# The pool of split weights opened after the pools of small tiles and activations

## The chip, the core and the metric

The program runs on one core of a Trainium2 chip. The metric is device time in microseconds (us) of one execution. The time of a kernel is the median of its timed runs; beside them stands one execution that was recorded by the profiler.

## What is computed

Two layers of a decoder trunk over 256 tokens of width 2048, in fp32. Layer 0 mixes by multi-head latent attention and a causal pooling mixer, layer 1 by a gated short convolution; each is followed by a squared-ReLU MLP of hidden width 8192.

```
for layer in range(2):
    h = rmsnorm(x, mix_norm_g[layer])
    if layer == 0:
        c_q, c_kv, k_rope, u_pool = split(h @ even_w_in)
        a = mla(c_q, c_kv, k_rope, ...)          # 8 heads, causal softmax
        b = pool_mixer(u_pool, ...)              # trailing means over 2/4/8/16 tokens
        x = x + concat([a, b]) @ even_w_out
    else:
        gate_b, gate_c, u = split(h @ odd_w_in)
        x = x + (gate_b * conv3(gate_c * u)) @ odd_w_out
    x = x + square(relu(rmsnorm(x, mlp_norm_g[layer]) @ w_mlp_up[layer])) @ w_mlp_down[layer]
```

## The kernel before

The weights come from HBM piece by piece, and every large product runs on TensorE. To keep fp32 accuracy with TensorE's fp32r operands, each weight and each activation is split in two halves, hi (the value rounded to fp32r) and lo (the rest), and a product is summed from hi·hi, hi·lo and lo·hi.

**The weights' way.** `slab` (L124) loads a piece of 1 MB, 128 partitions by 4 k-tiles by 512 columns, into a tile of the pool `raws` by a DMA that SyncE issues (L129). `halved` (L132) then cuts it into pieces of two k-tiles; for each, ScalarE writes the hi half (L141) and VectorE subtracts it from the raw weight and writes the lo half (L142). Both go to the pool `halves`, under the tags `hi` and `lo`, six buffers each, taken in turn. TensorE reads them in one of two roles: `columns_out` (L161, L162) has them as the stationary operand and streams the normed input `xT` past them, with 512 columns for hi and 256 for lo; `tokens_out` (L154 to L156) and the seven-product form of the MLP's second matrix (`down_seven`, L777 to L779) have an activation tile as the stationary operand and stream 512 columns of hi or lo.

**The activations.** `acts` holds four buffers of 8 KB a partition under the tag `hT` (`act_tile`); they carry the attention's and the MLP's activations, hi and lo, and at the start two of them, named `x0T`, hold the transposed input. The pool `small` has the short-lived tiles of VectorE and ScalarE: four buffers of 2 KB under the tag `t` (named junk, h, c, cu, b, y and so on), one named `f`, and statistics of a few bytes. `down_seven` also uses sums of activations, named `fT` by the profile, which lie in a pool of the MLP stage.

**Where pools lie.** A pool is a fixed stretch of each partition's on-chip memory (SBUF). The pools are stacked: each begins where the one opened before it ends, so the order in which they are opened sets the addresses. `const` and `big` are opened first, then the three pools of the change, then the pools of a stage (`raws` and others, through `new_stage`, L77). The attention's pool is stacked from the other end. The order of the instructions on each engine is that of the program text; the waits follow from which tiles an instruction reads and writes, and from which buffers are taken again.

```
    pools = dict(halves=ctx.enter_context(tc.tile_pool(name="halves", bufs=6)))
    small = ctx.enter_context(tc.tile_pool(name="small", bufs=2))
    T4 = dict(tag="t", bufs=4)
    acts = ctx.enter_context(tc.tile_pool(name="acts", bufs=4))
```

Of the kernel before, what the change touches and what calls it, by code (L numbers as in the profile page):

```python
# [67 lines left out]
def trunk(ctx: ExitStack, tc, x_in, xT_in, gains_in, pos_in, w_up, w_down, w_in, pool_in, w_uq, w_ukv,  # L68
# [16 lines left out]
                for name, bufs in wanted.items():  # L85
                    pools[name] = stage[-1].enter_context(tc.tile_pool(name=uid(name), bufs=bufs, reuse_waits="tile"))

    pools = dict(halves=ctx.enter_context(tc.tile_pool(name="halves", bufs=6)))
    small = ctx.enter_context(tc.tile_pool(name="small", bufs=2))
    T4 = dict(tag="t", bufs=4)  # L90
    acts = ctx.enter_context(tc.tile_pool(name="acts", bufs=4))
    psum = ctx.enter_context(tc.tile_pool(name="psum", bufs=4, space=PSUM))

    count = [0]
# [910 lines left out]
```

## Time and profile before

| | us |
|---|---|
| median of 3 runs (2029.35 to 2031.46) | 2030.74 |
| the profiled execution | 2031.15 |
| its span, first to last instruction | 2029.4 |
| TensorE (PE) matmuls busy in it | 2018.0 |
| VectorE (DVE) busy | 1395.3 |
| ScalarE (ACT) busy | 1120.8 |
| GpSimd (POOL) busy | 96.7 |

The 1.75 us between the profiled execution and its span lie around the first and the last instruction. In the profile's rows L161 is line 161 of the kernel, "ps<-xT,hi" names what an instruction writes and reads, PEld is TensorE's load of a stationary operand, and an engine's idle time is put down to what ended it.

### The profile page before, as it was taken

The numbers are of one execution on the slowest core, as the hardware profiler recorded it, in microseconds if no ns is written. First come the engines' busy times: TensorE is split into PE (matmuls) and PEld (weight loads), VectorE is DVE, ScalarE is ACT, GpSimd is POOL, SyncE is SP. The second block draws the span as 40 slices with busy tenths as digits, with TensorE's granted clock in tenths as the row PEclk, the third lists the DMA queues.
The fourth block names the chain that finished last, engine by engine and source line by source line (L and its number), as shares of the span: only waits on it lengthen the run. The fifth ranks groups of instructions, "written<-read, shape, count | busy, mean of one in ns | idle before, by whom it ended". The sixth has DMA issues, their size and how long they took to land.

```text
span 2029.4 us, 26720 instructions
## 1 busy us (share of the span) xinstructions
PE 2018.0 (99%) x10532; PEld 1722.8 (85%) x10532; DVE 1395.3 (69%) x1737; ACT 1120.8 (55%) x1480; POOL 96.7 (5%) x126
## 2 busy tenths in 40 slices
PE   8999999999999999999999999999999999999999
PEld 8987888888888888888888888888888888888887
DVE  6677567776777777676566656567776677767774
ACT  6576556655556555555444444456555565555552
POOL 1330000000000000000000000000000000000000
PEclk9999999999999999999999999999999999999999
DMA  8453758788878878665555557658797987879663
GB/s 316 157 203 130 241 179 237 256 251 262 272 236 265 256 239 270 230 208 187 184 184 188 186 185 242 213 177 248 236 282 245 274 235 260 257 250 283 197 216 124
DMA packets 67006, 459.72 MB, mean 227 GB/s; under 512 B 7280, under 2 KB 9760, under 8 KB 11968
## 3 DMA queue, kind: packets, MB, share of 16 engines
q1 hardware_dynamic: 58224, 397.89, 54.4%
q0 software_dynamic: 8224, 58.94, 15.3%
q8 instruction: 82, 1.34, 0.3%
q10 hardware_dynamic: 432, 1.18, 0.2%
q14 instruction: 44, 0.36, 0.0%
HBM read 455.89 MB, written 2.10 MB: 226 GB/s over the span
## 4 chain that ended last, share of the span: by engine, by line
PE 95%; DVE 1%; POOL 1%; DMA 1%; ACT 1%; issue 0%; ACTq 0%; DVEq 0%; POOLq 0%
PE ps L161 32%; PE ps L162 16%; PE ps L156 10%; PE ps L154 10%; PE ps L155 10%; PE ps L779 4%; PE ps L777 4%; PE ps L778 4%; POOL pn L489 1%; DVE lo L142 1%; PE ps L289 1%; DMA raw<-in_even_w_in 1%; ACT hi L141 0%; PE ps L618 0%; DMA raw<-in_even_w_out 0%
## 5 line engine op out<-in xcount | busy, mean ns | idle before, releaser
L142 DVE TENSOR_TENSOR lo<-raw,hi 128x1024 fp32r<-128x1024 f32 (+2 forms) x694 | 847.8, 1225 | 450.5 <-ACT hi L141 449.9
L141 ACT CAST hi<-raw 128x1024 fp32r<-128x1024 f32 (+2 forms) x694 | 724.2, 1046 | 620.7 <-PE ps L161 355.7
L161 PE MATMUL ps<-xT,hi 128*128 128x512 f32 x2816 | 997.3, 398 | 0.0
L162 PE MATMUL ps<-xT,lo 128*128 128x256 f32 x2816 | 790.5, 281 | 0.0
L161 PEld LDWEIGHTS ps<-xT,hi 128*128 128x128 f32 x2816 | 528.9, 188 | 129.4
L162 PEld LDWEIGHTS ps<-xT,lo 128*128 128x128 f32 x2816 | 532.0, 189 | 4.0
L154 PE MATMUL ps<-hi,hT 128*128 128x512 f32 (+1 forms) x896 | 351.3, 392 | 0.0
L156 PE MATMUL ps<-hi,hT 128*128 128x512 f32 (+1 forms) x896 | 350.3, 391 | 0.0
L155 PE MATMUL ps<-lo,hT 128*128 128x512 f32 (+1 forms) x896 | 348.0, 388 | 0.0
L156 PEld LDWEIGHTS ps<-hi,hT 128*128 128x128 f32 x896 | 168.4, 188 | 36.5
L155 PEld LDWEIGHTS ps<-lo,hT 128*128 128x128 f32 x896 | 168.3, 188 | 36.1
L154 PEld LDWEIGHTS ps<-hi,hT 128*128 128x128 f32 x896 | 168.4, 188 | 35.5 <-issue 1.3
L141 ACT CAST hi<-t 128x1024 fp32r<-128x1024 f32 x84 | 88.2, 1050 | 98.7 <-PE ps L161 51.5
L142 DVE TENSOR_TENSOR lo<-t,hi 128x1024 fp32r<-128x1024 f32 x84 | 102.6, 1222 | 46.3 <-ACT hi L141 45.3
L767 POOL DMA_DIRECT2D t<-in_w_mlp_down x42 | 36.7, 874 | 1153.6 <-DVE lo L142 746.6
L779 PE MATMUL ps<-hi,fT 128*128 128x512 f32 x224 | 88.0, 393 | 0.0
L778 PE MATMUL ps<-lo,fT 128*128 128x512 f32 x224 | 87.8, 392 | 0.0
L777 PE MATMUL ps<-hi,fT 128*128 128x512 f32 x224 | 87.7, 391 | 0.0
L779 PE MATMUL ps<-hi,hT 128*128 128x512 f32 x168 | 66.2, 394 | 0.0
L777 PE MATMUL ps<-hi,hT 128*128 128x512 f32 x168 | 65.9, 392 | 0.0
L778 PE MATMUL ps<-lo,hT 128*128 128x512 f32 x168 | 65.6, 391 | 0.0
L867 DVE SCALAR_TENSOR_TENSOR x<-ps,r,x 128x512 f32<-128x512 f32 (+1 forms) x73 | 50.9, 737 | 14.8 <-PE ps L156 14.8
(184 smaller groups left out, 1562.7 us busy)
## 6 DMA issues: line engine op xcount, KB each, us to landing
raw<-in_w_mlp_up SPq DMA_DIRECT2D x128, 1024.0 KB, 6.1
raw<-in_w_mlp_down SPq DMA_DIRECT2D x114, 1024.0 KB, 5.1
raw<-in_odd_w_in SPq DMA_DIRECT2D x48, 1024.0 KB, 4.9
t<-in_w_mlp_down POOLq DMA_DIRECT2D x42, 1024.0 KB, 9.4
raw<-in_even_w_out SPq DMA_DIRECT2D x16, 1024.0 KB, 5.0
raw<-in_odd_w_out SPq DMA_DIRECT2D x16, 1024.0 KB, 4.9
t<-in_w_mlp_down SPq DMA_DIRECT2D x14, 1024.0 KB, 4.8
v<-in_w_mlp_down SPq DMA_DIRECT2D x14, 1024.0 KB, 4.9
```

The costliest lines, as they stand in the source:

```text
L141: a = nc.scalar.copy(h, r)
L142: v = nc.vector.tensor_tensor(out=l, in0=r, in1=h.bitcast(F32), op=ALU.subtract)
L154: nc.tensor.matmul(o, lhsT=a_hi, rhs=hi[:, c0:c0 + n], start=first, stop=False)
L155: nc.tensor.matmul(o, lhsT=a_hi, rhs=lo[:, c0:c0 + n], start=False, stop=False)
L156: nc.tensor.matmul(o, lhsT=a_lo, rhs=hi[:, c0:c0 + n], start=False, stop=last)
L161: nc.tensor.matmul(o, lhsT=hi[:, c0:c0 + P], rhs=act[:, kt, :], start=first, stop=False)
L162: nc.tensor.matmul(o[:, S:2 * S], lhsT=lo[:, c0:c0 + P], rhs=act[:, kt, 0:S], start=False, stop=last)
L767: nc.gpsimd.dma_start(b, at(e, n), accum_op=ALU.add)
L777: nc.tensor.matmul(o, lhsT=a_hi, rhs=hi, start=q == 0, stop=False)
L778: nc.tensor.matmul(o, lhsT=a_hi, rhs=lo, start=False, stop=False)
L779: nc.tensor.matmul(o, lhsT=a_lo, rhs=hi, start=False, stop=q == 3)
L867: nc.vector.scalar_tensor_tensor(out=xb, in0=ps[:, t, :n], scalar=r2[0][:, t:t + 1], in1=xb, op0=ALU.mult, op1=ALU.add)
```

## The change

The line that opens `halves` moves behind the two that open `small` and `acts`.

```
-    pools = dict(halves=ctx.enter_context(tc.tile_pool(name="halves", bufs=6)))
     small = ctx.enter_context(tc.tile_pool(name="small", bufs=2))
     T4 = dict(tag="t", bufs=4)
     acts = ctx.enter_context(tc.tile_pool(name="acts", bufs=4))
+    pools = dict(halves=ctx.enter_context(tc.tile_pool(name="halves", bufs=6)))
     psum = ctx.enter_context(tc.tile_pool(name="psum", bufs=4, space=PSUM))
```

The sizes of the three pools stay, so the stretch that they fill together, bytes 67,360 to 163,039 of each partition, stays too, and with it every pool behind it. The built programs have the same instructions, in the same order on each of the five engines, with the same waits. Only the start addresses of the tiles in these three pools differ:

| pool | bytes a partition | starts at, before | starts at, after |
|---|---|---|---|
| `big`: the normed input xT (its last 32 KB) | 32,768 | 34,592 | 34,592 |
| `halves`: six hi | 26,112 | 67,360 | 110,816 |
| `halves`: six lo | 26,112 | 93,472 | 136,928 |
| `small` | 10,688 | 119,584 | 67,360 |
| `acts`: four hT | 32,768 | 130,272 | 78,048 |
| `raws` (first pool of a stage) | 24,576 | 163,040 | 163,040 |
| MLP stage: fT | 16,384 | 204,000 | 204,000 |

`halves` moves up by 43,456 bytes, `small` and `acts` move down by 52,224. All starts before and after are multiples of 32, and both distances are multiples of 64.

More of the change, by code (lines that the diff above doesn't have):

```diff
@@ L86, in new_stage @@
                     pools[name] = stage[-1].enter_context(tc.tile_pool(name=uid(name), bufs=bufs, reuse_waits="tile"))
-    pools = dict(halves=ctx.enter_context(tc.tile_pool(name="halves", bufs=6)))
     small = ctx.enter_context(tc.tile_pool(name="small", bufs=2))
@@ L91, in trunk @@
     acts = ctx.enter_context(tc.tile_pool(name="acts", bufs=4))
+    pools = dict(halves=ctx.enter_context(tc.tile_pool(name="halves", bufs=6)))
     psum = ctx.enter_context(tc.tile_pool(name="psum", bufs=4, space=PSUM))
```

## The prediction

> **What bounds the kernel now.** I read the page's busy times first, then the waits of TensorE alone, then busy time by stretch, and last the groups of instructions with shapes kept apart, for what a matmul, a split or a subtraction takes at different addresses. The first row is from the page, the next six are all the waits that the trace finds on PE, with total us, times and longest.
>
> ```profile
> PE 2018.0 (99%) x10532; PEld 1722.8 (85%) x10532; DVE 1395.3 (69%) x1737; ACT 1120.8 (55%) x1480; POOL 96.7 (5%) x126
> ...
> PE ps L154 <- ACT hi L141: 2.6, 1, 2.6
> PE ps L255 <- POOL ident masks.py:199: 2.5, 1, 2.5
> PE ps L610 <- DVE hT L205: 1.1, 1, 1.1
> PE ps L155 <- DVE lo L142: 0.9, 1, 0.9
> PE ps L167 <- ACT qkv L525: 0.4, 1, 0.4
> PE ps L167 <- DVE hT L205: 0.3, 1, 0.3
> ```
>
> Of the span of 2029.4 us the matmuls fill 2018.0. The waits sum to 7.8 us, 2.5 of them ahead of the first instruction; what is left of the 11.4, some 3.6 us, lies behind the last matmul. So TensorE streams without a break, and two things alone can move the end: the pace of the matmuls themselves, or another engine that becomes so slow that TensorE waits for it. Rows of busy time by stretch say how far off the second is. Their columns are us, then busy us and instructions of PE, PEld, DVE, ACT and POOL, then clock, DMA share and GB/s. The first row is the end of the latent projection, the second a piece of the first MLP, the third of the convolution's input product; the row below them counts L142 alone in the MLP piece.
>
> ```profile
> 20.00:60.00 40.00, 40.00 (x244) 40.00 (x243) 33.02 (x84) 26.45 (x43) 0.79 (x1) 1.00 0.76 286
> ...
> 400.00:600.00 200.00, 200.00 (x1014) 169.25 (x1013) 146.38 (x169) 114.13 (x130) 7.88 (x9) 1.00 0.81 253
> ...
> 980.00:1180.00 200.00, 200.00 (x1134) 173.33 (x1133) 124.90 (x150) 87.67 (x96) 0.62 (x6) 1.00 0.53 184
> ...
> 400.00:600.00 200.00, 108.22 (x90) 1.00 0.81 253
> ```
>
> PE is busy for all of each stretch, at a granted clock of 1.00. In the MLP, DVE has 53.6 us idle of 200 beside 90 subtractions of L142, so each could take 0.6 us more, 1.8 us in place of 1.2, before DVE filled the stretch.
>
> **The change, part by part.** It removes no instruction, adds none, moves none past another on any engine or DMA queue, and adds or takes no wait: the instruction lists of the two builds agree row for row. What changes is where the buffers of three pools lie: six hi, six lo, four hT and the small tiles. So the sum has one term for each kind of access to a moved buffer, the number of accesses times whatever the new address adds, and the question is whether an address has a price. The trace of before can answer that, since it has like instructions on buffers far apart. First TensorE, grouped with shapes kept apart (count, busy us, mean ns of one):
>
> ```profile
> L161 PE MATMUL ps<-xT,hi 128*128 128x512 f32 x2816 | 997.3, 398 | 0.0
> L162 PE MATMUL ps<-xT,lo 128*128 128x256 f32 x2816 | 790.5, 281 | 0.0
> ...
> L779 PE MATMUL ps<-hi,fT 128*128 128x512 f32 x224 | 88.0, 393 | 0.0
> L778 PE MATMUL ps<-lo,fT 128*128 128x512 f32 x224 | 87.8, 392 | 0.0
> L777 PE MATMUL ps<-hi,fT 128*128 128x512 f32 x224 | 87.7, 391 | 0.0
> L779 PE MATMUL ps<-hi,hT 128*128 128x512 f32 x168 | 66.2, 394 | 0.0
> L777 PE MATMUL ps<-hi,hT 128*128 128x512 f32 x168 | 65.9, 392 | 0.0
> L778 PE MATMUL ps<-lo,hT 128*128 128x512 f32 x168 | 65.6, 391 | 0.0
> ```
>
> Lines 777 to 779 run the same three matmuls with two different stationary tiles. hT lies at 130,272 to 163,039, fT at 204,000 to 220,383. Over all three lines fT takes (87.7+87.8+88.0)/672 = 392.1 ns and hT (65.9+65.6+66.2)/504 = 392.3 ns: 0.15 ns apart for a move of at least 41 KB, where the change moves hT by 52. The busy sums are rounded to 0.1 us, which blurs that by about as much again. The streamed operand shows the same: hi at 67,360 (L777) and lo at 93,472 (L778) are read at 391 to 392 ns. The loads of the stationary operand don't differ either, whether it is hi, hT or fT:
>
> ```profile
> L161 PEld LDWEIGHTS ps<-xT,hi 128*128 128x128 f32 x2816 | 528.9, 188 | 129.4
> ...
> L777 PEld LDWEIGHTS ps<-hi,fT 128*128 128x128 f32 x224 | 42.0, 188 | 9.9
> ...
> L777 PEld LDWEIGHTS ps<-hi,hT 128*128 128x128 f32 x168 | 31.5, 188 | 7.3 <-ACT hT L200 0.4
> ```
>
> Most places that are new for one kind of tile were used by PE before, for the other kind: the four hT come to 78,048 to 110,815, where hi and lo buffers stood, and all of lo comes to where hT stood. I take 0 for TensorE, and as bounds 0.3 ns to either side for each of the 10,532 matmuls (the 0.15 and its blur): 3.2 us less to 3.2 us more.
>
> Now the engines that write the buffers. ACT's split and DVE's subtraction, by source tile, and their writes to hT beside those to fT:
>
> ```profile
> L141 ACT CAST hi<-raw 128x1024 fp32r<-128x1024 f32 x676 | 707.0, 1048 | 607.7 <-PE ps L161 355.7 <-PE ps L156 123.7 <-PE ps L779 56.3
> ...
> L141 ACT CAST hi<-v 128x1024 fp32r<-128x1024 f32 x28 | 29.4, 1048 | 43.2 <-PE ps L161 23.5 <-DVE lo L142 19.7
> ...
> L200 ACT CAST hT<-h 128x512 fp32r<-128x512 f32 x64 | 39.7, 620 | 0.6
> ...
> L200 ACT CAST fT<-f 128x512 fp32r<-128x512 f32 x56 | 34.6, 618 | 9.6 <-DVE f L748 9.6
> ...
> L142 DVE TENSOR_TENSOR lo<-raw,hi 128x1024 fp32r<-128x1024 f32 x676 | 827.3, 1226 | 435.8 <-ACT hi L141 435.2
> ...
> L142 DVE TENSOR_TENSOR lo<-v,hi 128x1024 fp32r<-128x1024 f32 x28 | 34.3, 1225 | 33.9 <-ACT hi L141 33.9
> ...
> L201 DVE TENSOR_TENSOR hT<-h,hT 128x512 fp32r<-128x512 f32 x64 | 44.0, 687 | 1.1 <-ACT hT L200 0.7
> ...
> L201 DVE TENSOR_TENSOR fT<-f,fT 128x512 fp32r<-128x512 f32 x56 | 38.4, 685 | 0.0
> ```
>
> The largest difference by place is 2 ns in 600 or 700. Even if all 1,737 instructions of DVE took 2 ns more, that is 3.5 us spread over 2029, beside an idle time of 0.6 us at each subtraction, and ACT waits for PE far longer (607.7 us ahead of L141). Cost 0, covered by the matmuls; with no idle time to cover it, it would be those 3.5 us at most.
>
> One kind of DMA has a moved target, the loads of the transposed input into x0T at the start; what waited for them stands at the end of the row of their only reader on ACT:
>
> ```profile
> L204 ACT ACTIVATE xT<-x0T,gains 128x256 fp32r<-128x256 f32 x16 | 7.0, 498 | 1.0 <-DMA gains<-in_gains 0.8 <-DMA x0T<-in_xT 0.2
> ```
>
> They write the same bytes at another offset, and 0.2 us of waiting is put down to them; I take 0, with 0.2 us more or less as bounds. The DMAs into `raws`, all others of weight, have the targets they had.
>
> The sum: 2031.15 (the profiled execution: 2029.4 of span and 1.75 around it) + 0 = 2031.15 us. That execution is 0.41 us above the median of the runs, 2030.74, so the forecast in terms of a median is **2030.7 us**.
>
> The rows say that PE is not held up by what ACT, DVE and the DMAs do in the same memory: 200.00 us busy of 200.00 in an MLP stretch where they are busy for 114, 146 and 81%. The Trainium skill, in "SBUF — State Buffer", section "Who interferes with whom", has a rule of the same tenor: PE and ACT have ports of their own and never wait on anyone, the one shared pair of ports is that of DVE and GpSimd, and nothing in it goes by address along a partition. By that rule the first two rivals below would be worth 0 and the sum would stay 2031.15. The page speaks of ports, not of what lies behind them, so I leave the rivals some chance.
>
> **The rivals.**
>
> *Slower, by neighbours.* PE reads its stationary and its streamed operand at once. Suppose that costs more when the two lie close. After the change hT ends at 110,816, just where the hi buffers begin; before, 10.7 KB lay between lo's end and hT's start and 36.8 KB between hi's end and hT's. The nearest row for such a neighbourhood is L161: in it xT, which ends at 67,360, streams past hi, which before begins there, and it takes 398 ns against 391 for L777. If those 7 ns were the price and passed to the matmuls of hT with hi or lo (L154 to L156 with 896 each, L777 to L779 with 168 each, 3,192 in all), the time would be 2030.7 + 22.3 = **2053 us**. It decides from 4.1 us/3,192 = 1.3 ns a matmul, since PE has nothing to hide it under. Against it: hT and fT, at least 10 and 84 KB above the halves, differ by 0.15 ns; and L161 differs from L777 in other ways, as every second matmul there is a short one.
>
> *Faster, by the same mechanism.* L161 loses the neighbour: between xT and hi lie 43 KB after. If its 398 ns fell to 391, 2,816 × 7 = 19.7 us would go, to **2011 us**. Against it: the spread over all buffers and k-tiles of the other half of the pair, L162, is narrow. The row gives count, then min, median and max in ns:
>
> ```profile
> L162 PE MATMUL ps<-xT,lo x2816: 276/281/285, 270.8 to 1970.3; 128*128 128x256 f32 x188
> ```
>
> xT's nearest and farthest k-tile lie 30 KB apart and lo's buffers 22 KB, and all pairings together stay within 9 ns.
>
> *Slower, by DVE.* The lo buffers come to end at 163,040, where `raws` begins, and L142 reads one and writes the other. It decides from 1.8 us, where DVE fills the MLP. If neighbours doubled it, to 2.45 us, the 676 pieces read from raw would cost 827 us more; DVE has 2029.4 − 1395.3 = 634 us idle in all, so at least 193 us would be added, for **2224 us** or more. Against it: raw at 163,040 and v at 195,808 are read at the same 1225 to 1226 ns.
>
> *The change moves nothing.* If the allocator gave the same addresses, the time would be the same; the built addresses do differ, so it has no share of its own.
>
> **How the numbers follow.** No change: 0.88. Slower by neighbours: 0.06; slower by DVE: 0.01. Faster: 0.05. About 0.2%, 4.1 us, is what a measurement of this kernel can tell from no change, and the bound of 3.2 us stays inside it; so the chances are 0.05 faster, 0.88 the same, 0.07 slower. The range takes the bounds of 3.2 us and the spread of the runs around their median, 1.4 below and 0.7 above: 2030.7 − 4.6 = 2026.1 to 2030.7 + 3.9 = 2034.6. It leaves out the rivals, 0.12, and some of the rest.
>
> **What would show it.** L161 and L162 stay at 398 and 281 ns, L777 to L779 at 391 to 394 with both stationary tiles, the stationary loads at 188, L141 at 1048 and L142 at 1226, and PE's waits at about 8 us in the same six places. A matmul group of hT alone that is 1.3 ns or more longer shows the first rival; L161 alone shorter shows the second; new waits of PE for L142 show the third. If all groups are as before and the time still moved by more than 4 us, the argument that an address acts only through the length of the instructions is wrong.

## The result, and the profile after

| | before | after |
|---|---|---|
| median of 5 runs, us | 2030.18 (2029.35 to 2031.46) | 2018.58 (2017.77 to 2020.08) |
| ratio to before, 95% interval | | 0.9943 (0.9931 to 0.9954) |
| profiled execution, us | 2031.15 | 2020.08 |
| its span, us | 2029.4 | 2018.3 |
| PE matmuls busy, us | 2018.0 | 2007.2 |

The kernel became faster by 11.6 us, where no change was forecast. The forecast's range ended at 2026.1. The profile after, first the page's busy times, then all waits of PE:

```profile
PE 2007.2 (99%) x10532; PEld 1723.4 (85%) x10532; DVE 1394.9 (69%) x1737; ACT 1122.2 (56%) x1480; POOL 96.4 (5%) x126
...
PE ps L255 <- POOL ident masks.py:199: 2.5, 1, 2.5
PE ps L154 <- ACT hi L141: 2.0, 2, 1.1
PE ps L167 <- ACT qkv L525: 1.6, 1, 1.6
PE ps L155 <- DVE lo L142: 1.0, 2, 0.9
PE ps L167 <- DVE hT L205: 0.2, 1, 0.2
```

The waits sum to 7.3 us, as good as the 7.8 of before. The span lost 11.1 us and PE's busy time lost 10.8: TensorE still streams from end to end, it only needs less time for the same 10,532 matmuls. The granted clock doesn't explain that: it was 0.999 before and 0.998 after. The groups say which (count, busy us, mean ns of one):

```profile
L161 PE MATMUL ps<-xT,hi 128*128 128x512 f32 x2816 | 992.1, 394 | 0.0
L162 PE MATMUL ps<-xT,lo 128*128 128x256 f32 x2816 | 790.8, 281 | 0.0
L154 PE MATMUL ps<-hi,hT 128*128 128x512 f32 x880 | 344.6, 392 | 0.0
L156 PE MATMUL ps<-hi,hT 128*128 128x512 f32 x880 | 342.8, 390 | 0.0
L155 PE MATMUL ps<-lo,hT 128*128 128x512 f32 x880 | 342.5, 389 | 0.0
L777 PE MATMUL ps<-hi,fT 128*128 128x512 f32 x224 | 88.1, 393 | 0.0
L779 PE MATMUL ps<-hi,fT 128*128 128x512 f32 x224 | 87.7, 392 | 0.0
L778 PE MATMUL ps<-lo,fT 128*128 128x512 f32 x224 | 87.0, 389 | 0.0
L777 PE MATMUL ps<-hi,hT 128*128 128x512 f32 x168 | 65.8, 392 | 0.0
L779 PE MATMUL ps<-hi,hT 128*128 128x512 f32 x168 | 65.5, 390 | 0.0
L778 PE MATMUL ps<-lo,hT 128*128 128x512 f32 x168 | 65.4, 389 | 0.0
```

A row's busy time counts overlapping matmuls once. Every L161 begins before the last L161 has ended, so its busy time runs through: it is the length of the whole stream of pairs L161 and L162, and L162's isn't to be added. That stream is 5.2 us shorter (997.3 to 992.1). Before, the x880 rows of the three lines were 346.8, 345.8 and 343.5:

```profile
L154 PE MATMUL ps<-hi,hT 128*128 128x512 f32 x880 | 346.8, 394 | 0.0
L156 PE MATMUL ps<-hi,hT 128*128 128x512 f32 x880 | 345.8, 393 | 0.0
L155 PE MATMUL ps<-lo,hT 128*128 128x512 f32 x880 | 343.5, 390 | 0.0
```

So L154 to L156 went from 1036.1 to 1029.9, 6.2 us less, and L777 to L779 lost 0.7 (fT) and 1.0 (hT). That sums to 13.1 us; the span lost 11.1, as some small groups moved the other way and neighbouring groups overlap. The pace didn't change everywhere, though. L161 has 1,024 pairs in each MLP and 768 in the convolution's input product. Here are its rows in the first MLP (260 to 930 us) and in the convolution (930 to 1280 us), before and then after:

```profile
L161 PE MATMUL ps<-xT,hi 128*128 128x512 f32 x1024 | 362.9, 397 | 0.0
...
L161 PE MATMUL ps<-xT,hi 128*128 128x512 f32 x768 | 271.6, 399 | 0.0
```

```profile
L161 PE MATMUL ps<-xT,hi 128*128 128x512 f32 x1024 | 360.3, 394 | 0.0
...
L161 PE MATMUL ps<-xT,hi 128*128 128x512 f32 x768 | 271.6, 396 | 0.0
```

The second MLP has the rows of the first, 362.9 and 360.3. So the whole gain on pairs lies in the MLPs, 2.6 us in each, and the convolution's pairs take 271.6 us as before. DVE and ACT work as they did:

```profile
L142 DVE TENSOR_TENSOR lo<-raw,hi 128x1024 fp32r<-128x1024 f32 x676 | 827.1, 1226 | 429.1 <-ACT hi L141 428.3
...
L141 ACT CAST hi<-raw 128x1024 fp32r<-128x1024 f32 x676 | 708.3, 1050 | 599.7 <-PE ps L161 338.1 <-PE ps L156 115.2 <-PE ps L779 54.6
```

### The profile page after: what moved, and what is told of

Its sections match the earlier page's. It is cut to its first block, busy times and chain, and to the rows that moved or that the text cites. A ratio compares the mean times of both kernels' runs of the same rounds, so it can differ in the third digit from the quotient of the medians.

```text
span 2018.3 us, 26720 instructions
## 1 busy us (share of the span) xinstructions
PE 2007.2 (99%) x10532; PEld 1723.4 (85%) x10532; DVE 1394.9 (69%) x1737; ACT 1122.2 (56%) x1480; POOL 96.4 (5%) x126
## 4 chain that ended last, share of the span: by engine, by line
PE 96%; DVE 1%; POOL 1%; DMA 1%; ACT 1%; issue 0%; SPq 0%; ACTq 0%; DVEq 0%; POOLq 0%
PE ps L161 32%; PE ps L162 16%; PE ps L154 10%; PE ps L156 10%; PE ps L155 10%; PE ps L777 4%; PE ps L779 4%; PE ps L778 4%; DVE lo L142 1%; DMA raw<-in_even_w_in 1%; PE ps L289 1%; PE ps L167 0%; PE ps L169 0%; PE ps L168 0%; POOL pn L489 0%
## 5 line engine op out<-in xcount | busy, mean ns | idle before, releaser
L142 DVE TENSOR_TENSOR lo<-raw,hi 128x1024 fp32r<-128x1024 f32 (+2 forms) x694 | 847.6, 1225 | 444.4 <-ACT hi L141 443.5
L141 ACT CAST hi<-raw 128x1024 fp32r<-128x1024 f32 (+2 forms) x694 | 725.7, 1048 | 613.2 <-PE ps L161 338.1
L161 PE MATMUL ps<-xT,hi 128*128 128x512 f32 x2816 | 992.1, 394 | 0.0
L162 PE MATMUL ps<-xT,lo 128*128 128x256 f32 x2816 | 790.8, 281 | 0.0
L161 PEld LDWEIGHTS ps<-xT,hi 128*128 128x128 f32 x2816 | 529.4, 188 | 123.8
L162 PEld LDWEIGHTS ps<-xT,lo 128*128 128x128 f32 x2816 | 528.0, 188 | 3.6
L154 PE MATMUL ps<-hi,hT 128*128 128x512 f32 (+1 forms) x896 | 349.1, 390 | 0.0
L156 PE MATMUL ps<-hi,hT 128*128 128x512 f32 (+1 forms) x896 | 347.3, 388 | 0.0
L155 PE MATMUL ps<-lo,hT 128*128 128x512 f32 (+1 forms) x896 | 347.1, 387 | 0.0
L154 PEld LDWEIGHTS ps<-hi,hT 128*128 128x128 f32 x896 | 168.3, 188 | 35.0 <-issue 1.3
L156 PEld LDWEIGHTS ps<-hi,hT 128*128 128x128 f32 x896 | 168.3, 188 | 34.8
L155 PEld LDWEIGHTS ps<-lo,hT 128*128 128x128 f32 x896 | 168.4, 188 | 33.2
L141 ACT CAST hi<-t 128x1024 fp32r<-128x1024 f32 x84 | 88.5, 1053 | 92.7 <-PE ps L161 50.7
L142 DVE TENSOR_TENSOR lo<-t,hi 128x1024 fp32r<-128x1024 f32 x84 | 102.6, 1221 | 44.3 <-ACT hi L141 44.1
L777 PE MATMUL ps<-hi,fT 128*128 128x512 f32 x224 | 88.1, 393 | 0.0
L779 PE MATMUL ps<-hi,fT 128*128 128x512 f32 x224 | 87.7, 392 | 0.0
L777 PE MATMUL ps<-hi,hT 128*128 128x512 f32 x168 | 65.8, 392 | 0.0
L779 PE MATMUL ps<-hi,hT 128*128 128x512 f32 x168 | 65.5, 390 | 0.0
```

Of the source, the lines that this page charges most:

```text
L141: a = nc.scalar.copy(h, r)
L142: v = nc.vector.tensor_tensor(out=l, in0=r, in1=h.bitcast(F32), op=ALU.subtract)
L154: nc.tensor.matmul(o, lhsT=a_hi, rhs=hi[:, c0:c0 + n], start=first, stop=False)
L155: nc.tensor.matmul(o, lhsT=a_hi, rhs=lo[:, c0:c0 + n], start=False, stop=False)
L156: nc.tensor.matmul(o, lhsT=a_lo, rhs=hi[:, c0:c0 + n], start=False, stop=last)
L161: nc.tensor.matmul(o, lhsT=hi[:, c0:c0 + P], rhs=act[:, kt, :], start=first, stop=False)
```

## The experiments

Three theories, all on the length of matmuls. **Alignment**: what counts is the distance between the tile that PE streams and the stationary tile, modulo some power of two. Modulo 256 bytes, hi lay 0 above xT before and lies 192 above it after; against hT the distance was 64 and is 0; against fT also 64 and 0. **Place**: what counts is the gap in bytes, as in the prediction's first two rivals. **History**: PE's pace can settle in more than one way, and any disturbance tips it.

Fifteen kernels ran, all but one with the instructions of before in the same order, and only addresses changed, by another order of the pools or by unused bytes ("pad") between them. The table gives distances modulo 256, the median time, the busy time of L161, and the sums of the x880 rows of L154 to L156 and of the x224 rows of L777 to L779. (The expectations of the later runs count the short forms of L154 to L156 in, which adds 13.5 us: 1049.6 before, 1043.4 after.) The kernel of before, run beside them, had medians of 2029.4 to 2030.2.

| kernel | hi−xT | hi−hT | hi−fT | us | L161 | L154–156 | L777–779, fT |
|---|---|---|---|---|---|---|---|
| before | 0 | 64 | 64 | 2030.2 | 997.3 | 1036.1 | 263.5 |
| after | 192 | 0 | 0 | 2018.6 | 992.1 | 1029.9 | 262.8 |
| small, halves, acts | 192 | 0 | 0 | 2018.5 | 992.2 | 1029.9 | 262.9 |
| halves, acts, small | 0 | 0 | 64 | 2023.3 | 994.1 | 1029.9 | 263.5 |
| before, 192 in front | 192 | 64 | 64 | 2032.2 | 999.2 | 1035.4 | 263.8 |
| before, 256 in front | 0 | 64 | 64 | 2029.7 | 992.6 | 1035.3 | 263.5 |
| before, 64 ahead of acts | 0 | 0 | 0 | 2020.5 | 994.2 | 1029.6 | 263.0 |
| after, 64 in front | 0 | 0 | 0 | 2021.0 | 994.1 | 1029.6 | 263.0 |
| after, 128 in front | 64 | 0 | 0 | 2025.6 | 999.2 | 1029.9 | 263.2 |
| after, 32 in front | 224 | 0 | 0 | 2007.7 | 982.6 | 1029.9 | 262.4 |
| after, 32 ahead of halves | 224 | 32 | 0 | 2025.1 | 982.6 | 1044.3 | 262.5 |
| before, 224 in front, 32 ahead of acts | 224 | 32 | 32 | 2028.5 | 982.6 | 1044.3 | 264.7 |
| after, 32 in front, 32 between hi and lo | 224 (lo 0) | 0 (lo 32) | 224 (lo 0) | 2029.2 | 985.4 | 1044.2 | 265.1 |
| after, 96 in front | 32 | 0 | 0 | 2014.9 | 988.2 | 1030.2 | 263.4 |
| before, 224 in front, 64 ahead of acts | 224 | 0 | 0 | 2007.3 | 982.6 | 1029.9 | 262.4 |
| after, 160 in front | 96 | 0 | 0 | 2007.2 | 982.1 | 1029.6 | 261.8 |

The three right columns come from one profiled execution. At hi−xT 0 that was a long one for before and a short one for the four others; **By stage**, below, says what that makes of L161.

**Other orders.** The first kernel opens small, then halves, then acts:

```
     small = ...
+    pools = dict(halves=...)
     acts = ...
```

> Order small, halves, acts: acts and hT lie where they did before (130,272), halves start at 78,048. Alignment theory (what counts is the distance between the two operands of a matmul modulo 256 bytes: hi to xT was 0 and is 192 after the change, hi to hT was 64 and is 0 after it): both distances are here as after the change, so the time is 2018 to 2020 us, the busy sum of L161 and L162 about 1783 us as after (before 1788), that of L154 to L156 with hT about 1030 (before 1036). Place theory (the gap in bytes between tiles): the gap from xT to hi is 10,688 instead of 43,456 and the gap from lo to hT is 0, so L154 to L156 are not faster than before and the time stays above 2024 us. History theory (a small disturbance tips the pace of the matmul stream): any time from 2018 to 2031.

The profile of that kernel, its groups as above:

```profile
L161 PE MATMUL ps<-xT,hi 128*128 128x512 f32 x2816 | 992.2, 394 | 0.0
...
L154 PE MATMUL ps<-hi,hT 128*128 128x512 f32 x880 | 344.6, 392 | 0.0
L156 PE MATMUL ps<-hi,hT 128*128 128x512 f32 x880 | 342.8, 390 | 0.0
L155 PE MATMUL ps<-lo,hT 128*128 128x512 f32 x880 | 342.5, 389 | 0.0
```

With other places and gaps but the distances of after, it has the rows of after to 0.1 us, and the time (2018.5). Place is out for this pair, alignment is met. The second opens halves, acts, small:

```
     pools = dict(halves=...)
+    acts = ...
     small = ...
-    acts = ...
```

> Order halves, acts, small: halves stay where they were before, hT moves down by 10,688 bytes to 119,584. Alignment theory: hi to xT modulo 256 is 0 as before, so L161 and L162 keep their sum of 1788 us; hi to hT is 0 as after, so L154 to L156 with hT fall from 1036 to about 1030 us; time about 2023 to 2025 us. Place theory: nothing gained at L161, and lo now ends where hT begins, so 2030 us or more. History theory: any time from 2018 to 2031.

L154 to L156 fell to 1029.9 as alignment said, though hT had only moved down onto lo's end; the time was in its bounds, 2023.3. L161 was to stay at 997 and came out at 994.1. The kernel's runs lie in two groups, 2021.0 to 2021.6 and 2025.1 to 2027.7, and the profiled one is of the first.

**The old order with unused bytes in front.** 192 and 256 bytes:

```
+    pad = ctx.enter_context(tc.tile_pool(name="pad", bufs=1)).tile([P, 48], F32, name="pad")
     pools = dict(halves=...)
```

> The order of before with 192 unused bytes ahead of the halves, so that halves, small, acts and raws all move up by 192 against x and xT. Alignment theory: hi to xT becomes 192 as after, hi to hT stays at 64 as before: L161 and L162 fall to about 1783 us, L154 to L156 stay at 1036; time about 2025 us. Place theory: a gap of 192 bytes changes nothing, 2030 us. History theory: any time from 2018 to 2031.

> The same with 256 unused bytes. Alignment theory: all distances modulo 256 are those of before, 2030 us with L161 and L162 at 1788 and L154 to L156 at 1036 us. Place theory: 2030 us. History theory: any time from 2018 to 2031, and not bound to 2030.

With 256, all distances modulo 256 stay and so did the time (2029.7); L154 to L156 kept their length (1035.3). Its profile fell on a short execution, 2024.2 us, with L161 at 992.6, so for L161 history isn't out. With 192 alignment failed on L161: it was to fall to the 992 of after, and rose to 999.2; time 2032.2. L154 to L156 stayed near before (1035.4), as said. So hi−xT isn't all there is to L161: at 192 its stream takes 992.1 us in two kernels and 999.2 in a third, and in the kernel of after itself the convolution runs no faster than before. The difference lies in the MLPs, 363.8 us each here and 360.3 there. Place said 2030 for both and is off by 2 us for the first.

**Unused bytes that bring before to after, and after to before.**

```
     T4 = dict(tag="t", bufs=4)
+    pad = ctx.enter_context(tc.tile_pool(name="pad", bufs=1)).tile([P, 16], F32, name="pad")
     acts = ...
```

> The order of before, with 64 unused bytes between small and acts: halves stay, hT and fT move up by 64 bytes, so that hi to hT and hi to fT are 0 modulo 256, as after the change; hi to xT stays at 0, as before. Alignment theory: L154 to L156 with hT fall to 1043 us as after (before 1050), L777 to L779 with fT to 262.8; L161 and L162 stay near 1784 to 1788; time 2021 to 2027 us like the order halves, acts, small. Place theory (gaps and neighbours): 64 bytes change nothing, 2030 us. History theory (any disturbance tips the pace): L154 to L156 not bound to 1043.

> The order of after, with 64 unused bytes ahead of the three pools: hi to hT and hi to fT stay at 0; hi to xT goes from 192 to 0 modulo 256, as before the change. Alignment theory: L154 to L156 stay at 1043 us; the step of L162 goes back from 119 to 117 ns and the pairs of L161 and L162 run at 353 or 347 ns, not at 349; time 2021 to 2027 us. Place theory: 2018.6 us, as after.

In the first, the old order with 64 bytes ahead of acts, and the second, the new order with 64 bytes in front, the pools lie in different places and all three distances are 0. They took 2020.5 us, 0.5 under what was expected, and 2021.0. Their rows, first one, then the other:

```profile
L161 PE MATMUL ps<-xT,hi 128*128 128x512 f32 x2816 | 994.2, 397 | 0.0
...
L154 PE MATMUL ps<-hi,hT 128*128 128x512 f32 x880 | 344.5, 392 | 0.0
```

```profile
L161 PE MATMUL ps<-xT,hi 128*128 128x512 f32 x2816 | 994.1, 397 | 0.0
...
L154 PE MATMUL ps<-hi,hT 128*128 128x512 f32 x880 | 344.5, 392 | 0.0
```

Sixty-four bytes made the old kernel 9 us faster and the new one 2.4 us slower, and left the two with the same rows: place and order have no part here. In the profiled executions the span of the old kernel fell from 2029.4 to 2017.9 us. Moving hT and fT against the halves brought 8.0 of that (6.5 at L154 to L156, 0.5 and 1.0 at L777 to L779). Another 4.6 us is the convolution, whose pairs took 267.0 us in this execution, and the MLPs' pairs became slower, by 0.7 each.

**128 and 32 bytes in front of the new order**: a pad as above, opened ahead of the three pools.

> The same with 128 bytes: hi to xT is 64 modulo 256, and modulo 128 as after (64). Alignment theory with a period of 128 bytes: all steps as after, 2018.6 us. With a period of 256: a new pace of L161 and L162, neither that of before nor that of after; the rest as after. Place theory: 2018.6 us.

> The same with 32 bytes: hi to xT is 224 modulo 256. Alignment theory with a grain of 64 bytes or more: as after, 2018.6 us, or as 64 bytes; with a grain of 32 bytes or less: a pace of its own for L161 and L162. L154 to L156 stay at 1043 us in either case. Place theory: 2018.6 us.

With 128 the time was 2025.6 and L161 took 999.2 instead of 992.1. That speaks against a period of 128, though 192 had 999.2 as well in the old order; the triples with PE alone, below, settle it. With 32 it took 982.6 and the time fell to **2007.7 us**, 0.9893 of before (0.9878 to 0.9908): better than both kernels, and the grain is no coarser than 32 bytes. Its pairs in the convolution:

```profile
L161 PE MATMUL ps<-xT,hi 128*128 128x512 f32 x768 | 266.6, 390 | 0.0
```

That is 347 ns a pair, where before and after take 271.6 us or 354 ns.

**More distances.** 32 bytes ahead of the halves in the new order, which also moves them against hT; the same two distances in the old order; 32 bytes between hi and lo; 96 in front.

```
     acts = ctx.enter_context(tc.tile_pool(name="acts", bufs=4))
+    pad2 = ctx.enter_context(tc.tile_pool(name="pad2", bufs=1)).tile([P, 8], F32, name="pad2")
     pools = dict(halves=...)
```

> The order of after, with 32 unused bytes between acts and halves: hi to xT 224 modulo 256, the distance that gave 2007.7 us, and hi to hT 32 instead of 0. Alignment theory: L161 and L162 as with 32 bytes ahead (982.6 and 793.9 us); L154 to L156 get a new value, and if the loads of a stationary tile that lies 32 bytes below the streamed one on this circle are the good case for them too (as 224 is for L161), they fall below 1043 us; time 2004 to 2008 us. Place theory: as after, 2018.6 us.

> The order of before, with 224 unused bytes ahead of the halves and 32 between small and acts: hi to xT 224 and hi to hT 32 as in the kernel with 32 bytes between acts and halves (only hi to fT differs, 32 against 0). Alignment theory: the order of the pools plays no part, so L161, L162 and L154 to L156 have that kernel's times to 1 us, and the time is 2004 to 2009 us. Place theory: 2030 us, as before.

The hope that 32 would be good for L154 to L156 failed: they took 1044.3, 14.4 us more than at 0, and the time was 2025.1. But L161 took the 982.6 as said, and the kernel in the old order has both sums to 0.1 us. Its time was foretold as 2004 to 2009 on the same failed hope; it took 2028.5. Its median is 3.4 us above its twin's. In the profiled executions, whose spans differ by 1.5, L777 to L779 with fT, the distance in which the two differ, took 2.2 us more (264.7 against 262.5).

```
             hi = pools["halves"].tile([P, sub, cols], F32R, tag="hi", name=uid("hi"))
+            last_prep or pools["halves"].tile([P, 8], F32, tag="pad3", name="pad3", bufs=1)
             lo = pools["halves"].tile([P, sub, cols], F32R, tag="lo", name=uid("lo"))
```

> The order of after with 32 unused bytes ahead, and 32 more between the hi and the lo buffers: hi to xT 224 as in the 2007.7 us kernel, lo to xT 0. If what counts is the distance between the tile that PE streams and the stationary tile that it loads meanwhile for the next matmul, the step after L161 (lo is loaded while 512 columns of xT stream) goes from 229.0 to some 234 ns, as at distance 0, and the step after L162 (hi is loaded) stays near 118; time about 2018 to 2022 us. If only the tile of the running matmul counts, the step of L161 (hi) stays at 229 and that of L162 (lo) moves. If it is the distance of hi alone, nothing moves and the time is 2008 us.

This one was to tell whether the running matmul's own two tiles count, or the stream and the stationary tile loaded meanwhile for the next; the extra bytes are taken once, ahead of the lo buffers. It doesn't tell. The time, 2029.2, is none of those expected, since the shift of lo against hT, which the expectation left out, slowed L154 to L156 by 14.3 us. Against the kernel with 32 bytes in front, where the three rows are 342.7, 344.4 and 342.8:

```profile
L155 PE MATMUL ps<-lo,hT 128*128 128x512 f32 x880 | 350.7, 399 | 0.0
L154 PE MATMUL ps<-hi,hT 128*128 128x512 f32 x880 | 348.8, 396 | 0.0
L156 PE MATMUL ps<-hi,hT 128*128 128x512 f32 x880 | 344.7, 392 | 0.0
```

L155, which streams the shifted lo, lost most (8.0 us), but L154 and L156, whose tiles are still at 0, lost 4.4 and 1.9. A delay that is handed on to the neighbours would fit; no run shows that. L161 moved by 2.8 us, which no version said, and not the same way everywhere: the convolution's pairs went from 266.6 to 271.3, the MLPs' from 358.0 to 357.1 each. The runs lie in two groups, 2022.5 to 2023.2 (three) and 2028.9 to 2031.2 (seven), and the profiled one is of the second.

> The order of after with 96 unused bytes ahead: hi to xT 32 modulo 256, a value not yet seen; hi to hT 0. Alignment theory: L154 to L156 stay at 1043 us; L161 and L162 take a pace of their own, between the best (982.6 and 793.9 us at 224) and the worst (999.2 and 791.4 us at 64). Place theory: 2018.6 us.

L161 at 988.2 lies between best and worst, with the other rows near those of after; 2014.9 us. It isn't a pace between the two, but a mix: the MLPs' pairs take 358.3 us each, nearly as at 224 (358.0), the convolution's 271.6, as before.

**PE alone.** The kernel of before with 712 us of matmuls behind its last one, in the two forms, for eight distances, each twice. It was executed once:

```
     mlp(1, ss, xT)
+    for again in range(2):
+        for kw in run(pair, 0, 64): nc.tensor.matmul(kw.pop("out"), **kw)
...
+        for kw in run(triple, 224, 32): nc.tensor.matmul(kw.pop("out"), **kw)
```

> The kernel of before, with matmuls added behind the last one, when DVE, ACT, GpSimd and the DMAs have nothing more to do: for each distance of 0, 32, ... 224 bytes between the stationary and the streamed tile, 64 pairs in the form of L161 and L162 and 32 triples in the form of L154 to L156, all twice; their result is not used. If the pace comes from PE's own two reads (the stationary load and the stream), the pairs follow the kernels: about 349 to 353 ns at 0, 353 at 64, 347 at 224, 349 at 192, and the triples about 227 ns a matmul at 0, 230 at 64 and 234 at 32. If it comes from writes of ACT, DVE or the DMAs that happen to lie at such a distance, all eight distances run alike here. The time is longer than before by the added work, about 2 x 8 x (22.4 + 22.1) = 712 us.

Line 974 is the pairs at distance 0, 975 at 32 and so on to 981; 982 to 989 are the triples. The first row is a stretch of the added part (PE, PEld, DVE, ACT, POOL, clock, DMA share, GB/s), the others the groups; their busy time is that of two runs of 64 pairs, or of two runs of 96 matmuls.

```profile
2048.00:2068.00 20.00, 20.00 (x115) 17.40 (x114) 0.00 (x0) 0.00 (x0) 0.00 (x0) 1.00 0.00 0
...
L974 PE MATMUL ps<-flat 128*128 128x512 f32 (+1 forms) x256 | 45.6, 340 | 0.0
L975 PE MATMUL ps<-flat 128*128 128x512 f32 (+1 forms) x256 | 45.6, 339 | 0.0
L980 PE MATMUL ps<-flat 128*128 128x512 f32 (+1 forms) x256 | 45.5, 339 | 0.0
L976 PE MATMUL ps<-flat 128*128 128x512 f32 (+1 forms) x256 | 45.5, 339 | 0.0
L987 PE MATMUL ps<-flat 128*128 128x512 f32 x192 | 45.3, 396 | 0.0
L978 PE MATMUL ps<-flat 128*128 128x512 f32 (+1 forms) x256 | 45.3, 338 | 0.0
L985 PE MATMUL ps<-flat 128*128 128x512 f32 x192 | 45.1, 395 | 0.0
L983 PE MATMUL ps<-flat 128*128 128x512 f32 x192 | 45.1, 395 | 0.0
L979 PE MATMUL ps<-flat 128*128 128x512 f32 (+1 forms) x256 | 45.1, 336 | 0.0
L986 PE MATMUL ps<-flat 128*128 128x512 f32 x192 | 45.1, 395 | 0.0
L989 PE MATMUL ps<-flat 128*128 128x512 f32 x192 | 45.1, 395 | 0.0
L988 PE MATMUL ps<-flat 128*128 128x512 f32 x192 | 45.1, 395 | 0.0
L981 PE MATMUL ps<-flat 128*128 128x512 f32 (+1 forms) x256 | 44.7, 336 | 0.0
L977 PE MATMUL ps<-flat 128*128 128x512 f32 (+1 forms) x256 | 44.7, 336 | 0.0
L984 PE MATMUL ps<-flat 128*128 128x512 f32 x192 | 44.3, 391 | 0.0
L982 PE MATMUL ps<-flat 128*128 128x512 f32 x192 | 43.9, 389 | 0.0
```

No other engine and no DMA works beside these matmuls, and the distances still differ: the pairs need 45.5 to 45.6 us at 0, 32, 64 and 192, 45.1 to 45.3 at 128 and 160, and 44.7 at 96 and 224, that is 0.9 us or 7 ns a pair between worst and best. The triples need 43.9 at 0, 44.3 at 64 and 45.1 to 45.3 at every other distance: 1.2 to 1.4 us, 6 to 7 ns a matmul. So no other engine and no DMA is the cause: the lines differ in the address of one tile that PE reads. They also differ in the output buffer, one of four taken in turn, and 96 and 224 share one; the kernels, below, settle that. A period of 128 is out, as the triples need 43.9 at 0 and 45.1 at 128. At 192 the pairs run like those at 0, as they did in the old order with 192 in front; the better pace at 192 of the kernel of after didn't appear here.

**Two last checks.** The old order with the three distances of the fastest kernel (224 in front, 64 ahead of acts), and the new order with 160 in front, which makes hi−xT 96, a distance that had run only with PE alone.

> The order of before, with 224 unused bytes ahead of the halves and 64 between small and acts: hi to xT 224, hi to hT 0, hi to fT 0, the same three distances as the 2007.7 us kernel, which had the order of after and 32 bytes. If the distances are the whole cause, it runs at 2007 to 2009 us with L161, L162 and L154 to L156 at 982.6, 793.9 and 1043.4 us. If the order of the pools has a share of its own, it stays some microseconds above.

> The order of after with 160 unused bytes ahead: hi to xT 96, hi to hT and hi to fT 0. With PE alone the pairs ran at 346.7 ns at 96 as at 224, so the time is that of the 2007.7 us kernel to 2 us, and L161 plus L162 near 1776 us. If the pace with PE alone doesn't carry over, the time lies at the 2014 to 2026 us of the other distances.

Both did as said. The old order has the fast kernel's rows and 2007.3 us, 0.9891 of before (0.9876 to 0.9906):

```profile
L161 PE MATMUL ps<-xT,hi 128*128 128x512 f32 x2816 | 982.6, 391 | 0.0
L162 PE MATMUL ps<-xT,lo 128*128 128x256 f32 x2816 | 793.9, 282 | 0.0
L154 PE MATMUL ps<-hi,hT 128*128 128x512 f32 x880 | 344.4, 391 | 0.0
```

So the order that the change sets has no share of its own. The other took 2007.2 us with L161 at 982.1; L161 plus L162 came to 1769.5 where 1776 was said, nearly all of it in L162's row, which overlaps L161's.

**By stage.** The rows of L161 in the convolution and in one MLP, beside PE alone (us):

| hi−xT | convolution, 768 pairs | MLP, 1,024 pairs | PE alone, 128 pairs |
|---|---|---|---|
| 0 | 271.6 (before), 266.9 to 267.0 (four others) | 362.9 (hi−hT 64), 363.5 to 363.6 (hi−hT 0) | 45.6 |
| 32 | 271.6 | 358.3 | 45.6 |
| 64 | 271.7 | 363.8 | 45.5 |
| 96 | 266.6 | 357.7 | 44.7 |
| 192 | 271.6 to 271.7 | 360.3 (hi−hT 0), 363.8 (hi−hT 64) | 45.5 |
| 224 | 266.6 | 358.0 | 44.7 |

In the convolution nothing comes between the pairs, and they have two paces: 353 or 354 ns, and 347 or 348 ns. At 96 and 224 they are fast and at 32, 64 and 192 slow, as with PE alone; no pad moves the outputs, so those aren't the cause. At 0 either happens. The twin of before with 256 in front has the MLPs of before to 0.1 us and this row in the convolution (its line 162 is 161 of the others), against 271.6:

```profile
L162 PE MATMUL ps<-xT,hi 128*128 128x512 f32 x768 | 266.9, 394 | 0.0
```

These 4.7 us are the whole step between long and short executions in L161. In the MLPs, where the pairs alternate with L777 to L779 and L154 to L156, 32 is fast and 192 went with hi−hT. So the 5.2 us that the change gains on pairs follow the new addresses (three kernels with hi−xT 192 ran, and the two with hi−hT 0 have them), but the rule behind them stays open.

One rival can't be told apart for the pairs. xT starts at byte 34,592 in every kernel, and the tile of PE alone stands in its place. So hi−xT is also the stationary tile's own start modulo 256, less 32, and 96 and 224 are the cases in which that tile starts at a multiple of 128 bytes. For L154 to L156 the distance it is: at hi−hT 0 they take 1029.6 to 1030.2 us with hi starting at 0, 32, 64, 96, 128 or 224 modulo 256, and with hi at 32 they take 1036.1 or 1029.9 as hT lies 64 or 0 from it.

## Why the prediction was wrong

**What bounds the kernel** was right, and is why the miss was not hidden: PE streams without a break, its waits stayed at 7 to 8 us, and every ns of a matmul shows in the time.

**"I take 0 for TensorE, and as bounds 0.3 ns to either side"** is the step that failed. Measured: the pairs lost 5.2 us, all of it over the 2,048 of the MLPs, 2.5 ns each, and L154 to L156 lost 6.2 us over 2,640, 2.3 ns each, far outside the bound. The bound rested on rows that could not show the effect. hT and fT, compared as two tiles far apart, lay at the same distance from hi modulo 256: 67,360 − 130,272 = −246·256 + 64 and 67,360 − 204,000 = −534·256 + 64. hi and lo are 102·256 bytes apart, and the six buffers of a tag lie 17·256 apart. Both comparisons set a case beside its repeat, so their likeness, 392.1 against 392.3 ns, said nothing of the change, which moved the distances from 0 to 192 and from 64 to 0. The table of start addresses held all that was needed to see this. The spread was too narrow as well: three runs gave 1.4 us below the median, and later runs of before itself came out as low as 2024.6, under the range.

**ACT, DVE and the DMA at 0**: right; L141, L142 and the waits stand as they stood.

**The rule of the Trainium skill** that PE never waits on anyone ("SBUF — State Buffer", section "Who interferes with whom"; it counts two read ports for PE, one for the stream and one for the load, as independent) spoke for 0. That no other engine holds PE up agrees with the convolution, whose pairs, with DVE, ACT and DMAs at work, are fast and slow at the distances where they are so with PE alone (at 0 either). But with PE alone the same triples took 43.9 or 45.1 us by the distance of their two tiles, so "independent" doesn't hold for the time, and the measurement decides.

**The rivals.** "Faster, by the same mechanism" had the direction and one of the places, L161 at 394 instead of 398. That was luck, since its mechanism fell: a gap of 192 bytes made L161 slower, one of 256 left the median alone, and one of 10,688 did what 43,456 did. It also had nothing on L154 to L156, from which the larger part came. "Slower, by neighbours" named those lines, and they became faster with the gap closed. "Slower, by DVE" showed nowhere.

**The test that was set** separated the cases rightly: the groups did change, so an address acts here through the length of the matmuls and not in some other way.

## What to carry to other kernels

Where PE streams without a break, as here, try the addresses of its two operands as a tuning knob: 32 unused bytes took this kernel from 2018.6 to 2007.7 us. Compare starts modulo 256 bytes, not gaps, read a row by stage before a rule is drawn from it, and when a trace is used to show that something has no price, check first that its cases differ in the thing at issue. A gain from moving a pool or a buffer may have nothing to do with the order that was chosen; a scan of a few pads finds out.

## What the runs showed of the hardware

- The pace of a stream of matmuls goes by where its stationary and streamed tiles start modulo 256 bytes, and a step of 32 bytes shows. With PE alone the best distances (stationary minus streamed) for pairs of 512 and 256 columns are 96 and 224 (44.7 us against 45.1 to 45.6); for triples of 512 columns (streamed minus stationary) 0, then 64 (43.9, then 44.3 against 45.1 to 45.3). For triples it is the distance that counts; for pairs the start of the stationary tile alone would fit as well. Why is open: the runs show no bank or port, only the pace.
- The same addresses can run at two paces. The kernel of before, run 25 times beside the first four kernels, took 2028.9 to 2031.5 us 21 times and 2024.6 to 2026.2 four times. The profile of its twin with 256 bytes in front fell on a short execution (span 2022.4 us), and there L161 is shorter, 992.6 against 997.3, all of it in the convolution, with L154 to L156 nearly alike (1035.3 against 1036.1). What decides between the paces was not tried. Whether it is also behind the two results at 192 stays open. The runs of each of the three kernels at 2007 us stayed within 2.8 us.
